# The last 32 adaLN blocks as float32 matmuls on TensorE, moved to other places, and activation tiles of 1 KB

## The chip, the cores and the metric

The kernel runs on one core of a Trainium2 chip. TensorE multiplies into PSUM (eight banks of 128 x 512 float32), VectorE and ScalarE work on PSUM and SBUF, GpSimd on SBUF, and SyncE issues the loads from memory. The time is device microseconds from launch to end, the median of several executions, and lower is better. A profiled execution gives the trace that is read below.

## The reference

One decoder block on 256 tokens of 1,024 channels: an adaLN modulation from a condition vector `c`, a normalisation, one wide input projection that feeds two mixers (native sparse attention and gated DeltaNet), their merge, an output projection, and a gated feed-forward with a short convolution. The part that the change touches is the first line:

```python
mod = (c @ w_ada[l] + b_ada[l])[:, None, :]              # 6 x 1024 numbers from c (1024)
sh_m, sc_m, gt_m, sh_f, sc_f, gt_f = jnp.split(mod, 6, axis=-1)
h = rms_norm(x, norm_mix[l]) * (1.0 + sc_m) + sh_m
q_a, kv_a, gl_a, qkv_b, a_b, b_b, z_b, merge = jnp.split(h @ w_in[l], split_at, axis=-1)
y_a = nsa_attention(q_a, ...)
y_b = gated_deltanet(qkv_b, a_b, b_b, z_b, ...)
mixed = g_a * (y_a @ w_proj_nsa[l]) + g_b * (y_b @ w_proj_gdn[l])
x = x + gt_m * (mixed @ w_out[l])
h = rms_norm(x, norm_ffn[l]) * (1.0 + sc_f) + sh_f
x = x + gt_f * ((jax.nn.silu(u_gate) * u_val) @ ffn_down[l])   # u: up-projection and conv of h
```

So `mod` is one matrix-vector product, 1,024 by 6,144. Its first third (sh_m, sc_m) is wanted at once; gt_m at the residual behind `w_out`, sc_f and shf at the second normalisation, gt_f at the very end.

## The kernel before, in words

Activations lie with channels on partitions, as eight pieces of 128 channels by 256 tokens. Every weight matrix comes in tiles of 128 x 1,024 float32 (512 KB) through five raw slots (tag `wraw`). Each is split: ScalarE casts it to `whi` (line 242), VectorE or GpSimd subtracts to get `wlo` (line 243). A projection `lin` takes two such tiles and makes 48 matmuls of 128 x 256, three for each of 16 products (lines 265, 267, 268), into one of three PSUM banks of tag `lin`.

The stages in program order: the modulated norm with the k and q projections of the DeltaNet (until about 100 us); the DeltaNet's preparation with v and query projections; keys, values and the compression for the attention, among them the z projections `gates_z`; the attention loop `scores` / `probs` / `trans` / `values` over 16 heads, beside which the delta rule's steps (`inverse`, `delta`) run; eight projections for the merge gates `mg`; eight output projections `pn` and `pg` of the two mixers; four of `w_out` (source tile `mxh`); and the feed-forward: `up` projections, convolutions, `down` matmuls (`dn`, lines 1127 to 1129).

The 6,144 numbers of `mod` are made in 48 blocks of 128. A block is one 512 KB load into a raw slot (line 209) and one VectorE instruction with a fused sum (line 213), which multiplies it with `c` spread over all partitions. Sixteen blocks stand in the first stage. The others are placed by the table `ADA`: a count for each z projection, each merge-gate projection, each output projection, one number for each `w_out` projection, and the first feed-forward step from which eight single blocks follow.

Apart from the very start (`manual_schedule`), the order of the instructions on each engine is made by a list scheduler when the program is built. It takes the program order as priority, simulates the engines, and lets a later stage's work move ahead wherever its inputs, its buffers and its engine are free; that is how projections come to lie among the attention's steps. Every tag is a ring of buffers: an instruction that writes a new tile waits for a free one. SyncE issues loads strictly in its order, so a load that waits for its slot holds the loads behind it. `big` makes the activation tiles of tag `b8`: eight pieces in one tile, two tiles in the ring (`hh` and `hl`, then `mxh` and `mxl`, then `fh` and `fl`).

Of the kernel before, what the change touches and what calls it, by code (L numbers as in the profile page):

```python
# [12 lines left out]
F32R = mybir.dt.float32r  # L13
# [3 lines left out]
ALU = mybir.AluOpType  # L17
# [4 lines left out]
P = 128  # L22
D = 1024
KB = D // P
T = 256
# [20 lines left out]
QG = 1  # L46
ADA = ([0] * 4, [1] * 8, [1] * 8, 2, 4)
WARM = (2, 4)
# [4 lines left out]
for _name, _w in (("bada", 48), ("nmix", 8), ("nffn", 8), ("nfin", 8), ("conv", 96), ("fconv", 132),  # L53
                  ("fconvb", 44), ("gnorm", 1), ("ckb1", 2), ("cvb1", 2), ("ckb2", 1),
                  ("posk", 16), ("posv", 16), ("rows", 80)):
    COLS[_name] = (_n, _n + _w)
    _n += _w
# [44 lines left out]
def build(tc, a, probe=None):  # L102
    nc = tc.nc
    V, S, G, TE = nc.vector, nc.scalar, nc.gpsimd, nc.tensor
    with ExitStack() as ctx:
# [11 lines left out]
        def big(name):  # L117
            t = wk.tile([P, KB, T], F32R, name=name, tag="b8", bufs=2)
            return [t[:, k] for k in range(KB)]

# [33 lines left out]
        start = ExitStack()  # L154
# [57 lines left out]
        def adasum(m, w):  # L212
            V.tensor_tensor_reduce(w, w, cb, 1.0, cl("bada", m), ALU.mult, ALU.add, mod[:, m:m + 1])  # L213

        def ada(n=1):

            for _ in range(n):
                m = next(mods)
                adasum(m, adaload(m))

# [753 lines left out]
        for i in range(18):  # L974
            if i < 15:
                queries(i + 1)
            if i < 16:
                scores(*divmod(i, 4))
            if 1 <= i <= 16:
                probs(*divmod(i - 1, 4))  # L980
                if i % 4 == 0:
                    compressed(i // 4 - 1)
            if i >= 2:
                trans(*divmod(i - 2, 4))
                if i % 4 == 1:
                    values((i - 2) // 4)
# [196 lines left out]
def layout(x, c, w_ada, b_ada, norm_mix, w_in, nsa_pos_k, nsa_pos_v, nsa_ck_w1, nsa_ck_b1, nsa_ck_w2, nsa_ck_b2,  # L1183
# [8 lines left out]
    order = [b for k in range(8) for b in (8 + k, k)] + [*range(16, 24), *range(32, 40), *range(24, 32), *range(40, 48)]  # L1192
    wa = np.asarray(w_ada)[0].T.reshape(48, P, D)[order]
    d["ada"] = f(wa)
    ba = np.asarray(b_ada)[0].reshape(48, P)[order].T

    def pairs(w):
# [30 lines left out]
                                  chan(np.asarray(nsa_cv_b1)[0]), np.tile(np.asarray(nsa_ck_b2)[0], 2)[:, None],  # L1228
                                  pos(nsa_pos_k), pos(nsa_pos_v), np.broadcast_to(rows, (P, 80))], 1))
    d["const"] = constants()  # L1230
# [15 lines left out]
```

## Time and profile before

| | us |
|---|---|
| median of 3 runs | 658.89 (656.87 to 660.06) |
| profiled execution, its own time | 659.57 |
| its span, first to last instruction | 657.4 |
| TensorE busy | 594.0 |
| VectorE busy | 521.7 |
| ScalarE busy | 381.9 |
| GpSimd busy | 342.6 |

In the rows below PE is TensorE's matmuls, PEld its weight loads, DVE VectorE, ACT ScalarE, POOL GpSimd, SP SyncE. A row of a window gives its start and end in us, its length, then for each engine the busy time and in brackets the number of instructions, the granted TensorE clock (1.00 is full), the busy share of the DMA engines and the GB/s moved. A row of a group gives line, engine, operation, output and inputs by name, shapes and type, the count, then the busy time in us and the mean ns of one, and the idle time of the engine in front of it with what ended it. A float32 matmul is recorded as two passes.

### The profile page before, as it was taken

The page shows a single profiled execution, that of the slowest core. Times are in us where ns is not written, and L with a number is a line of the kernel's source. Part 1 is how long each engine was busy: PE and PEld are TensorE (multiplying, and loading weights), DVE is VectorE, ACT ScalarE, POOL GpSimd, SP SyncE. Part 2 cuts the span into 40 slices and gives each one's busy share as a digit, 9 for nine tenths or more (in the row PEclk, how much of TensorE's full clock was granted, in tenths as well). Part 3 has the DMA queues.
Part 4 walks back from the last instruction along what each step waited for, and adds up shares of the span by engine and source line. Part 5 has one row for each costly group of instructions (what it writes and reads, how often), then busy time and mean ns, then how long its engine had stood idle before and what let it go on. Part 6 is the DMA issues. An engine that isn't in the chain of part 4 may idle for free.

```text
span 657.4 us, 13689 instructions
## 1 busy us (share of the span) xinstructions
PE 594.0 (90%) x5128; PEld 560.1 (85%) x5128; DVE 521.7 (79%) x1209; ACT 381.9 (58%) x855; POOL 342.6 (52%) x239
## 2 busy tenths in 40 slices
PE   7888999899998988999899899698876989999994
PEld 4887899788998877999887898698866989999994
DVE  5989859789999998697967889779997577575645
ACT  4324997744565586596786542566554565555443
POOL 3324797735675777364622363456642276644431
PEclk9999999999998999899999999799996999999998
DMA  7788666344695644233432557764776556363501
GB/s 289 247 295 319 216 203 207 105 154 133 194 290 192 229 159 140 88 97 130 160 99 66 167 203 254 273 225 132 243 221 238 174 204 198 131 224 130 193 1 64
DMA packets 35363, 119.72 MB, mean 182 GB/s; under 512 B 4961, under 2 KB 5729, under 8 KB 35298
## 3 DMA queue, kind: packets, MB, share of 16 engines
q1 hardware_dynamic: 35298, 118.86, 53.7%
q8 instruction: 40, 0.66, 0.4%
q14 instruction: 25, 0.20, 0.1%
HBM read 117.66 MB, written 1.18 MB: 181 GB/s over the span
## 4 chain that ended last, share of the span: by engine, by line
PE 39%; DVE 34%; DMA 11%; ACT 7%; issue 5%; POOL 2%; SPq 1%; DVEq 0%; ACTq 0%; POOLq 0%
DMA wada<-in_ada 8%; PE lin L265 8%; PE lin L268 8%; PE lin L267 8%; DVE wada L213 7%; DVE wlo L243 5%; PE dn L1128 3%; PE dn L1129 3%; PE dn L1127 2%; ACT whi L242 2%; POOL wlo L243 2%; DVE pp L921 2%; DVE cacc L397 1%; DVE pp L905 1%; DVE fl L1101 1%
## 5 line engine op out<-in xcount | busy, mean ns | idle before, releaser
L243 POOL TENSOR_TENSOR wlo<-wraw,whi 128x1024 fp32r<-128x1024 f32 x90 | 230.4, 2569 | 177.1 <-ACT whi L242 84.5
L242 ACT CAST whi<-wraw 128x1024 fp32r<-128x1024 f32 x144 | 149.9, 1048 | 79.3 <-PE lin L267 23.6
L265 PE MATMUL lin<-hh,whi 128*128 128x256 f32 x384 | 112.0, 292 | 1.0 <-DVE cacc L397 0.7
L268 PE MATMUL lin<-hh,wlo 128*128 128x256 f32 x384 | 111.5, 291 | 0.0
L267 PE MATMUL lin<-hl,whi 128*128 128x256 f32 x384 | 111.4, 290 | 0.0
L213 DVE CUSTOM_DVE_ANT_0 wada<-wada,cb,col 128x1024 f32<-128x1024 f32 x48 | 84.8, 1768 | 15.3 <-DMA wada<-in_ada 15.3
L243 DVE TENSOR_TENSOR wlo<-wraw,whi 128x1024 fp32r<-128x1024 f32 x54 | 84.2, 1560 | 7.3 <-ACT whi L242 6.1
L265 PE MATMUL lin<-fh,whi 128*128 128x256 f32 x304 | 86.7, 286 | 3.0 <-DVE al L252 3.0
L267 PE MATMUL lin<-fl,whi 128*128 128x256 f32 x304 | 86.8, 286 | 1.8 <-DVE fl L1101 1.8
L268 PE MATMUL lin<-fh,wlo 128*128 128x256 f32 x304 | 86.7, 285 | 1.3 <-DVE wlo L243 1.3
L265 PEld LDWEIGHTS lin<-hh,whi 128*128 128x128 f32 x384 | 74.6, 194 | 1.9 <-ACT whi L242 0.8
L268 PEld LDWEIGHTS lin<-hh,wlo 128*128 128x128 f32 x384 | 74.6, 195 | 0.8 <-issue 0.3
L267 PEld LDWEIGHTS lin<-hl,whi 128*128 128x128 f32 x384 | 74.5, 194 | 0.6
L265 PEld LDWEIGHTS lin<-fh,whi 128*128 128x128 f32 x304 | 58.8, 194 | 3.4 <-DVE al L252 3.4
L267 PEld LDWEIGHTS lin<-fl,whi 128*128 128x128 f32 x304 | 58.9, 194 | 2.3 <-DVE fl L1101 2.3
L268 PEld LDWEIGHTS lin<-fh,wlo 128*128 128x128 f32 x304 | 58.9, 194 | 1.5 <-DVE wlo L243 1.5
L243 POOL TENSOR_TENSOR dlo<-wraw,dhi 128x1024 fp32r<-128x1024 f32 x14 | 36.1, 2583 | 44.9 <-ACT dhi L242 42.3
L1127 PE MATMUL dn<-ah,dhi 128*128 128x256 f32 x176 | 48.4, 285 | 6.2 <-ACT ah L251 6.2
L1128 PE MATMUL dn<-al,dhi 128*128 128x256 f32 x176 | 49.7, 284 | 3.7 <-DVE al L252 3.7
L1129 PE MATMUL dn<-ah,dlo 128*128 128x256 f32 x176 | 49.1, 281 | 0.0
L1127 PEld LDWEIGHTS dn<-ah,dhi 128*128 128x128 f32 x176 | 33.2, 193 | 6.9 <-ACT ah L251 6.8
L1128 PEld LDWEIGHTS dn<-al,dhi 128*128 128x128 f32 x176 | 34.0, 193 | 4.4 <-DVE al L252 4.4
(410 smaller groups left out, 1608.3 us busy)
## 6 DMA issues: line engine op xcount, KB each, us to landing
wraw<-in_win SPq DMA_DIRECT2D x52, 512.0 KB, 3.7
wada<-in_ada SPq DMA_DIRECT2D x48, 512.0 KB, 4.5
wraw<-in_up SPq DMA_DIRECT2D x44, 512.0 KB, 4.3
wraw<-in_down SPq DMA_DIRECT2D x22, 512.0 KB, 4.0
wraw<-in_wko SPq DMA_DIRECT2D x16, 512.0 KB, 5.3
wraw<-in_pn SPq DMA_DIRECT2D x8, 512.0 KB, 4.2
wraw<-in_pg SPq DMA_DIRECT2D x8, 512.0 KB, 3.7
wraw<-in_wo SPq DMA_DIRECT2D x8, 512.0 KB, 4.1
```

Source lines behind the costliest of these rows:

```text
L213: V.tensor_tensor_reduce(w, w, cb, 1.0, cl("bada", m), ALU.mult, ALU.add, mod[:, m:m + 1])
L242: recent[S] = S.copy(hi, w).ins
L243: recent[e] = e.tensor_tensor(lo, w, hi.bitcast(F32), op=ALU.subtract).ins
L265: TE.matmul(o[:, b], hi[:, j, cs], hh[k], start=k == 0 and b == 0, stop=False, skip_group_check=True)
L267: TE.matmul(o[:, b], hi[:, j, cs], hl[k], start=False, stop=False, skip_group_check=True)
L268: TE.matmul(o[:, b], lo[:, j, cs], hh[k], start=False, stop=k == KB - 1 and b == blocks - 1, skip_group_check=True)
L397: V.scalar_tensor_tensor(acc[:, sft:], src[:, :T - sft], col[:, w0 + 3 - sft:w0 + 4 - sft], acc[:, sft:], op0=ALU.mult, op1=ALU.add)
L905: V.tensor_tensor_reduce(ap[0], src, ap[1], 0.125, -3e38, ALU.add, ALU.max, mx[:, 1 + w, t, r:r + 1])
L921: (G if 2 * w + t in POOLP else V).tensor_scalar(pv, pv, wt[:, 1 + w, t, r:r + 1], None, op0=ALU.mult)
L1127: TE.matmul(o, hi[:, cs], ah, start=f == 0 and b % 2 == 0, stop=False, skip_group_check=True)
L1128: TE.matmul(o, hi[:, cs], al, start=False, stop=False, skip_group_check=True)
L1129: TE.matmul(o, lo[:, cs], ah, start=False, stop=f == NF - 1 and b % 2 == 1, skip_group_check=True)
```

## The change

Blocks 16 to 47 are no longer summed by VectorE. `adapart` multiplies a block on TensorE in eight float32 matmuls: the stationary operand is one column of `c` spread over 32 columns, the moving one a 128 x 128 piece of the block, and the output goes to one of four strips of 32 partitions, each strip taking two of the eight. ScalarE copies the 128 x 128 result to SBUF, a second float32 matmul with a selecting column adds the four strips and turns the row into a column, and VectorE adds the bias. The bank is one of the three of tag `lin`; the copy `adt` lies in the ring `th` (16 buffers), which the delta rule's steps use too. On the host the weights of those 32 blocks are transposed, and nine columns (`c` and the selector) join the constants.

The places change as well: one block behind each head's `scores` (16), none at the merge gates and at `w_out`, eight at the output projections and eight in the feed-forward as before. And `big` makes eight tiles of 1 KB per partition with 16 in the ring, where it made one of 8 KB with two.

```diff
--- before.py
+++ after.py
@@ -44,7 +44,7 @@
 PARTS = 2
 OUTS = {0: 0, 1: 1, 3: 2, 5: 4, 7: 6}
 QG = 1
-ADA = ([0] * 4, [1] * 8, [1] * 8, 2, 4)
+ADA = ([0] * 4, [0] * 8, [1] * 8, 0, 4)
 WARM = (2, 4)
 GC = math.sqrt(2.0 / math.pi)
 
@@ -52,7 +52,7 @@
 _n = 0
 for _name, _w in (("bada", 48), ("nmix", 8), ("nffn", 8), ("nfin", 8), ("conv", 96), ("fconv", 132),
                   ("fconvb", 44), ("gnorm", 1), ("ckb1", 2), ("cvb1", 2), ("ckb2", 1),
-                  ("posk", 16), ("posv", 16), ("rows", 80)):
+                  ("posk", 16), ("posv", 16), ("rows", 80), ("cc", 8), ("sel", 1)):
     COLS[_name] = (_n, _n + _w)
     _n += _w
 NCOLS = _n
@@ -115,8 +115,7 @@
             return ps.tile(list(shape), F32, name=name, tag=tag, bufs=PB[tag])
 
         def big(name):
-            t = wk.tile([P, KB, T], F32R, name=name, tag="b8", bufs=2)
-            return [t[:, k] for k in range(KB)]
+            return [wk.tile([P, T], F32R, name=name, tag="b8", bufs=16) for _ in range(KB)]
 
         TAGS = {"mg": (46, 256), "ma": (24, 256), "mz": (24, 256), "tc": (8, 256), "tg": (10, 256), "ta": (4, 256),
                 "th": (16, 128), "t2": (3, 512), "yf": (3, 512), "qq": (2, 512), "lb": (4, 1024), "mk": (2, 1024), "mf": (1, 1024), "dh": (8, 1024), "t4": (6, 1024)}
@@ -216,7 +215,18 @@
 
             for _ in range(n):
                 m = next(mods)
-                adasum(m, adaload(m))
+                (adapart if m >= 16 else adasum)(m, adaload(m))
+
+        def adapart(m, w):
+
+            o, t = bank("ad", "lin"), tl("adt", "th")
+            for k in range(KB):
+                q = 32 * (k % 4)
+                TE.matmul(o[q:q + 32, :P], cl("cc", k).to_broadcast([P, 32]), w[:, k * P:k * P + P], start=k < 4,
+                          stop=k >= 4, skip_group_check=True)
+            S.copy(t, o[:, :P])
+            TE.matmul(o[:, P:P + 1], t, cl("sel", 0), start=True, stop=True, skip_group_check=True)
+            V.tensor_tensor(mod[:, m:m + 1], o[:, P:P + 1], cl("bada", m), op=ALU.add)
 
         mods = itertools.count(2)
 
@@ -976,6 +986,7 @@
                 queries(i + 1)
             if i < 16:
                 scores(*divmod(i, 4))
+                ada()
             if 1 <= i <= 16:
                 probs(*divmod(i - 1, 4))
                 if i % 4 == 0:
@@ -1191,6 +1202,8 @@
 
     order = [b for k in range(8) for b in (8 + k, k)] + [*range(16, 24), *range(32, 40), *range(24, 32), *range(40, 48)]
     wa = np.asarray(w_ada)[0].T.reshape(48, P, D)[order]
+
+    wa[16:] = wa[16:].reshape(32, P, KB, P).transpose(0, 3, 2, 1).reshape(32, P, D)
     d["ada"] = f(wa)
     ba = np.asarray(b_ada)[0].reshape(48, P)[order].T
 
@@ -1226,7 +1239,8 @@
                                   chan(norm_final), conv, fcv, chan(np.asarray(ffn_conv_b)[0]),
                                   chan(np.asarray(gdn_norm)[0]), chan(np.asarray(nsa_ck_b1)[0]),
                                   chan(np.asarray(nsa_cv_b1)[0]), np.tile(np.asarray(nsa_ck_b2)[0], 2)[:, None],
-                                  pos(nsa_pos_k), pos(nsa_pos_v), np.broadcast_to(rows, (P, 80))], 1))
+                                  pos(nsa_pos_k), pos(nsa_pos_v), np.broadcast_to(rows, (P, 80)), chan(np.asarray(c)[0]),
+                                  (np.arange(P)[:, None] % 32 == 0).astype(np.float32)], 1))
     d["const"] = constants()
     return d
 
```

What the built program makes of it is shown at three places. In the new file the lines behind the new function have numbers 10 or 11 higher.

TensorE, right behind the last matmuls of the compression (`hp`), where the attention begins; `lin` is a projection's bank, here for z and the merge gates. Before:

```order
L809 MATMUL hp<-whi,mk_2880 128x256
L810 MATMUL hp<-wlo,mk_2880 128x256
L265 MATMUL lin<-hh,whi 128x256
L267 MATMUL lin<-hl,whi 128x256
L265 MATMUL lin<-hh,whi 128x256
L267 MATMUL lin<-hl,whi 128x256
L268 MATMUL lin<-hh,wlo 128x256
L265 MATMUL lin<-hh,whi 128x256
L267 MATMUL lin<-hl,whi 128x256
L268 MATMUL lin<-hh,wlo 128x256
L265 MATMUL lin<-hh,whi 128x256
L267 MATMUL lin<-hl,whi 128x256
```

And with the change; `ad` is a block's bank, `ht` belongs to the compression, `s` holds a head's scores:

```order
L819 MATMUL hp<-whi,mk_2894 128x256
L820 MATMUL hp<-wlo,mk_2894 128x256
L225 MATMUL ad<-wada,col 32x128 x22
L827 MATMUL ht<-cst,hs 128x64 x2
L904 MATMUL s_3515<-KS,qq 128x272 x2
L904 MATMUL s_3515<-KS,qq 128x16 x2
L225 MATMUL ad<-wada,col 32x128 x2
L904 MATMUL s_3516<-KS,qq 128x512 x2
L904 MATMUL s_3551<-KS,qq 128x272 x2
L904 MATMUL s_3551<-KS,qq 128x16 x2
L850 MATMUL ht<-w_709,xr 96x64 x2
L904 MATMUL s_3552<-KS,qq 128x512 x2
```

Three blocks (24 matmuls) stand where projections stood. From here to the end of the delta rule the new order has no row of `lin` on TensorE; the old one has 480 such matmuls of `hh` and `hl` and 48 of the first output projections among the same steps. In the new order thirteen more blocks follow the delta rule's last matmul, and then the 480.

ScalarE, in the attention: `pp` are the softmax's probabilities, `mg` the merge gates out of their bank, `whi` a weight tile's cast. Before, in the middle:

```order
L914 ACTIVATE pp,misc<-pp,misc 128x128
L914 ACTIVATE pp,misc<-pp,misc 128x256
L914 ACTIVATE pp,misc<-pp,misc 128x128
L914 ACTIVATE pp,misc<-pp,misc 128x256
L881 CAST qq<-qT_835 64x256 x2
L242 CAST whi<-wraw 128x1024
L914 ACTIVATE pp,misc<-pp,misc 128x128
L914 ACTIVATE pp,misc<-pp,misc 128x256
L914 ACTIVATE pp,misc<-pp,misc 128x128
L914 ACTIVATE pp,misc<-pp,misc 128x256
L997 ACTIVATE mg_4478<-lin 128x256
L997 ACTIVATE mg_4479<-lin 128x256
```

And with the change at the attention's end, where its first rows of `adt` stand; `vn` and `sq` are the last steps of the delta rule, `oT` its output:

```order
L717 COPY vn_2663<-d_2696 128x128
L717 COPY vn_2664<-d_2696 128x128
L727 ACTIVATE sq,misc<-oT_2671 128x128
L261 CAST ya_3498<-y 128x256
L261 CAST ya_3500<-y 128x256
L261 CAST ybh_5250<-yb 128x256
L727 ACTIVATE sq,misc<-oT_2671 128x128
L727 ACTIVATE sq,misc<-oT_2672 128x128 x2
L227 COPY adt<-ad 128x128 x3
L261 CAST ybh_5251<-yb 128x256
L261 CAST ybh_5252<-yb 128x256
L261 CAST ybh_5253<-yb 128x256
```

The first copy out of a block's bank stands behind the delta rule's last squares. No cast of a weight tile stands between the first `pp` and there.

SyncE, from the last loads of the compression (`cvw`) on. Before:

```order
L230 DMA wraw<-in_cvw 128x1024 x3
L230 DMA wraw<-in_win 128x1024 x6
L209 DMA wada<-in_ada 128x1024
L230 DMA wraw<-in_win 128x1024 x2
L209 DMA wada<-in_ada 128x1024
L230 DMA wraw<-in_win 128x1024 x2
L209 DMA wada<-in_ada 128x1024
L230 DMA wraw<-in_win 128x1024 x2
L209 DMA wada<-in_ada 128x1024
L230 DMA wraw<-in_win 128x1024 x2
```

And with the change:

```order
L240 DMA wraw<-in_cvw 128x1024 x3
L208 DMA wada<-in_ada 128x1024 x8
L150 DMA x_5987<-in_x 128x512 x2
L150 DMA x_5988<-in_x 128x512 x2
L208 DMA wada<-in_ada 128x1024 x8
L240 DMA wraw<-in_win 128x1024 x20
L240 DMA wraw<-in_pn 128x1024 x2
L208 DMA wada<-in_ada 128x1024
```

Sixteen block loads, with the second load of `x` between them, stand ahead of all 20 tiles for z and the merge gates, where they alternated with them one to two.

## Rows read from the trace of the kernel before

**Rows 1.** The page: span, busy time of two engines, chain by engine.

```profile
span 657.4 us, 13689 instructions
PE 594.0 (90%) x5128; PEld 560.1 (85%) x5128; DVE 521.7 (79%) x1209; ACT 381.9 (58%) x855; POOL 342.6 (52%) x239
...
PE 39%; DVE 34%; DMA 11%; ACT 7%; issue 5%; POOL 2%; SPq 1%; DVEq 0%; ACTq 0%; POOLq 0%
```

**Rows 2.** Windows by stage, from the attention on.

```profile
208.00:358.00 150.00, 138.67 (x1594) 125.37 (x1594) 127.39 (x460) 105.77 (x334) 85.10 (x99) 0.98 0.42 138
358.00:403.00 45.00, 42.52 (x363) 41.87 (x361) 40.24 (x67) 20.76 (x40) 22.03 (x9) 1.00 0.57 188
403.00:425.00 22.00, 15.80 (x100) 14.32 (x101) 17.46 (x26) 7.29 (x9) 6.85 (x3) 0.84 0.82 281
425.00:465.00 40.00, 36.82 (x298) 36.03 (x297) 34.48 (x56) 25.19 (x52) 24.73 (x14) 1.00 0.50 163
465.00:535.00 70.00, 57.01 (x435) 55.19 (x434) 55.36 (x75) 36.00 (x56) 31.82 (x13) 0.93 0.64 213
535.00:657.00 122.00, 113.97 (x962) 113.31 (x961) 73.11 (x119) 64.67 (x110) 53.42 (x22) 0.98 0.42 146
```

**Rows 3.** Windows of 10 us, in the attention and behind it.

```profile
225.00:235.00 10.00, 8.53 (x96) 7.96 (x96) 9.94 (x35) 7.29 (x23) 9.46 (x8) 1.00 0.54 191
255.00:265.00 10.00, 7.32 (x85) 4.98 (x83) 7.33 (x20) 5.39 (x18) 6.53 (x7) 0.85 0.51 160
265.00:275.00 10.00, 10.00 (x138) 9.52 (x137) 6.46 (x22) 3.75 (x11) 3.48 (x8) 0.81 0.18 54
295.00:305.00 10.00, 10.00 (x161) 8.70 (x160) 6.46 (x24) 4.44 (x14) 4.77 (x8) 1.00 0.46 159
375.00:385.00 10.00, 10.00 (x87) 9.89 (x86) 8.26 (x14) 5.66 (x9) 3.38 (x2) 1.00 0.51 165
405.00:415.00 10.00, 5.29 (x41) 4.68 (x39) 7.46 (x15) 3.68 (x5) 2.76 (x2) 1.00 0.86 302
```

**Rows 4.** The chain in order of time around 410 us: start, us, what.

```profile
402.94 3.33 DVE wada L213
...
409.27 5.49 DMA wada<-in_ada
...
414.88 1.28 DVE wada L213
```

**Rows 5.** Groups of TensorE by form, 208 to 358 us.

```profile
L268 PE MATMUL lin<-hh,wlo 128*128 128x256 f32 x159 | 46.5, 294 | 0.0
...
L265 PE MATMUL lin<-ya,whi 128*128 128x256 f32 x13 | 3.9, 301 | 0.0
```

**Rows 6.** VectorE's blocks: all of them (page), and those of 358 to 535 us.

```profile
L213 DVE CUSTOM_DVE_ANT_0 wada<-wada,cb,col 128x1024 f32<-128x1024 f32 x48 | 84.8, 1768 | 15.3 <-DMA wada<-in_ada 15.3
...
L213 DVE CUSTOM_DVE_ANT_0 wada<-wada,cb,col 128x1024 f32<-128x1024 f32 x20 | 37.9, 1897 | 9.1 <-DMA wada<-in_ada 9.1
```

**Rows 7.** Groups of VectorE by form, 208 to 358 us: blocks, weight splits.

```profile
L213 DVE CUSTOM_DVE_ANT_0 wada<-wada,cb,col 128x1024 f32<-128x1024 f32 x12 | 15.9, 1328 | 1.8 <-DMA wada<-in_ada 1.8
L243 DVE TENSOR_TENSOR wlo<-wraw,whi 128x1024 fp32r<-128x1024 f32 x10 | 14.7, 1472 | 0.2 <-ACT whi L242 0.2
```

**Rows 8.** DMA issues (page): count, KB of each, median us from issue to landing.

```profile
wada<-in_ada SPq DMA_DIRECT2D x48, 512.0 KB, 4.5
```

**Rows 9.** TensorE in order of time: start, us from first to last, what, count.

```profile
351.11 0.83 PE L697 MATMUL d<-St,kq 128*128 128x128 f32 x6
351.88 2.81 PE L967 MATMUL y<-pt,VV 128*64 128x256 f32 x30
```

**Rows 10.** Waits of TensorE, 375 to 560 us: total us, times, longest.

```profile
PE dn L1127 <- ACT ah L251: 6.2, 3, 3.9
PE lin L265 <- ACT mxh L251: 5.4, 3, 3.7
```

## The prediction

> **What bounds the kernel now.** I read the page first, then the stages one by one, the groups of instructions in two of them, and the waits and the chain last. Over the span TensorE is busy 90% and VectorE 79%, and both carry the chain of waits (39% and 34%) [rows 1]: neither is the bound alone, so the question is which of them limits which stage. The stages answer it [rows 2]. A projection runs at 87 matmuls in 10 us, 0.115 us each, with TensorE fully busy (375 to 385 in [rows 3]); that is the pace of a stage bound by TensorE. By it, 358 to 403 (363 matmuls, 42 of 45 us) and the tail from 535 (962, 111 of 122 us) are TensorE's. But 403 to 425 has 100 matmuls (11.5 us) in 22 us, and 465 to 535 has 435 (50 us) in 70 us: there TensorE waits, with VectorE busy 55.4 of 70 us, and the chain alternates between adaLN blocks, their loads and weight splits [rows 4]. The attention, 208 to 358, is of a third kind. Its matmuls are 475 of the merge-gate and z projections (three lines of 158 or 159, of which one is shown) and 39 of the first output projection (three lines of 13) [rows 5], laid between the steps of the softmax and of the delta rule. The attention's own chains leave holes; the projections fill them. In a slice such as 295 to 305 TensorE is at 10 of 10 and VectorE at 6.5; in 225 to 235 VectorE is at 9.9 [rows 3].
>
> **What the change does to the order.** The price lies here, less in the arithmetic. Taking a block off VectorE saves 1.77 us of it, 32 times, 57 us [rows 6]. But in the new order the first three blocks of the attention are multiplied ahead of everything, and each keeps one of the three banks of tag "lin" until ScalarE has copied it and VectorE has read the second product. ScalarE's first three copies stand behind the last square of the delta rule, at the attention's end. Every merge-gate and z projection needs a "lin" bank, so none can run in between. On SyncE the second blocks hold the five raw-weight slots as well, so nothing can be loaded ahead. All 480 projection matmuls of that kind follow the attention.
>
> **The terms**, against the profiled execution (span 657.4 us, time 659.57 us, so 2.2 us lie around it; the median 658.89 us is 0.1% below, which I ignore).
>
> *A. The attention without its filler.* The 514 matmuls leave the 150 us and cost 514 x 0.115 = 59 us elsewhere. What is left of VectorE there is 127.4 - 15.9 (blocks) - 14.7 (weight splits) = 96.8 us [rows 2, 7]; TensorE keeps about 139 - 59 = 80 us. At VectorE's present share of the stage (127.4 of 150, 85%) the rest takes 114 us; at the 99% of its best slice, 98 us. I take 110: near the first, as the delta steps still wait in turn, with a little off because TensorE's queue no longer holds foreign matmuls and GpSimd stops splitting weights. A = 110 + 59 - 150 = +19 us. The low end is 98, so +7. The high end: the granted clock fell to 0.81 in 265 to 275, after a slice with TensorE busy 7.3 of 10 [rows 3]; VectorE's work with all of today's idle time (22.6 us) is 119 us, and TensorE's 80 us become 99 at 0.81; if those 19 us come on top, the attention takes 138 us, +47.
>
> *B. Blocks that wait until the attention is over.* Thirteen remain; five lie loaded, eight of 512 KB must be fetched, then two raw tiles before a projection starts. At the best rate that this kernel shows, 302 GB/s [rows 3], a tile takes 1.74 us: ten tiles 17.4 us, and a first landing (4.5 us median [rows 8]) of which about half passes while the loaded blocks run. I take +20 us with little else on TensorE. Low end 12 us, TensorE's own work at 0.9 us a block; high end 26 us, if the three-bank rounds (products, copies, second products, additions) don't overlap with the loads, or the loads of x (1 MB, 3.5 us), which now stand between the two groups of eight blocks on SyncE, hold the second group back.
>
> *C. Eight blocks among the output projections*, a stretch that TensorE paces. What a block costs has to be bounded. Two strips of 64 columns run side by side in the value product: 3,072 columns of float32 in 2.8 us, 0.9 ns a column [rows 9]; a block's 8 x 128 columns would take 0.92 us. Four strips could halve that (0.46); a single one costs 0.11 us for each of two recorded passes of 128 columns (the first line of [rows 9]), so 1.8 us if the strips don't overlap. I take 0.9, the row that does the like: +7 us (4 to 14).
>
> The Trainium skill, "TensorEngine Tiling (Array Packing)", Key Properties, says that changing the tiling mode drains the engine. The rows don't show it: the first strip product starts at 351.88 us, before the modelled end of the full-width products ahead (351.11 + 0.83) [rows 9]. By the rule, with a drain of one 0.28 us matmul, two switches for each of 16 blocks would add an estimated 9 us to C and E; by the rows, nothing, and the sum goes by the rows.
>
> *D. The wait ahead of the w_out projection.* 403 to 425 loses 22 - 11.5 = 10.5 us; the chain there is a block (3.3 us), a block's load (5.5) and another block (1.3) [rows 4]. TensorE waits for mxh, 5.4 us [rows 10]; a part stays, as mxh's last pieces need the last projection. -7 us (-3 to -9).
>
> *E. The start of the feed-forward.* 425 to 465 gives back some 1 us (0 to 3). 465 to 535 loses 20 us; VectorE's eight blocks there cost it some 15 us at the 1.9 us mean of that part of the kernel [rows 6], and TensorE's waits for ah, 6.2 us, follow from its lag [rows 10]. I give back 11 (5 to 14), since the convolutions stay. The eight blocks now cost TensorE 8 x 0.9 = 7 us (4 to 14).
>
> *Nothing* for the rest. The 1 KB tiles let mxh or fh be written piece by piece as hh or mxh is released; but mxh's first piece comes after the merge-gate projections anyway, and fh waits for the norm's sum over all of w_out. A gain is bounded by D's wait (5.4 us), a loss by nothing larger than one release. The nine extra constant columns ride in a load that is there. The three blocks ahead of the attention (2.8 us) take the place of 36 projection matmuls (4.1 us) that stood ahead of the first scores. The copies on ScalarE and the additions of one column on VectorE lie beside TensorE's work: ScalarE is busy 20.8 of 45 us among the output projections, 36 of 70 in the feed-forward's start [rows 2].
>
> Sum: 19 + 20 + 7 - 7 - 1 - 11 + 7 = +34 us; 657.4 + 34 + 2.2 = 694 us.
>
> **Rivals.**
> 1. *A milder loss*: the attention falls to VectorE's floor, loads and blocks overlap, four strips run at once, and VectorE's relief is given back in full. All low ends together are 7 + 12 + 4 - 9 - 3 - 14 + 4 = +1, so 661 us; halfway to my sum it is 677 us. For it: VectorE's 9.9 slices. Against: the delta steps' waits, and slots that are freed one by one.
> 2. *A dearer one*: TensorE at a low clock through the emptier attention and strips that don't overlap. With A +47, B +26, C and E's blocks 14 each, and the rest as taken (-7 - 1 - 11) the sum is +82, 742 us; it begins where half of that excess is there, at 717 us. For it: the 0.81 clock. Against: TensorE keeps 80 us of work there, and two strips did overlap. The Trainium skill, "TensorE: Matmul & The Clock Gate", Part 1, has the gate close on idleness; no row here has so thin an attention.
> 3. *Faster*: VectorE's relief decides. Its place is everything behind the attention and the attention itself, where blocks and GpSimd's splits slow its other work (a block takes 1.33 us there and 1.90 us later [rows 6, 7]). With the other terms at their good ends (12 + 4 - 9 - 3 - 14 + 4 = -6), the kernel wins from the point where the attention takes less than 150 - 59 + 6 = 97 us, just under today's 96.8 us of VectorE work. At 90 us it gives 652 us. Against: every term has to come out well at once, and 80 us of TensorE work sit in the same chains.
>
> **How the numbers follow.** Forecast 0.63 (677 to 717), rival 1 0.18, rival 2 0.12, rival 3 0.07. Rival 1 lies almost wholly above 662 us, so slower by over 0.5% (what a measurement of this kernel can tell from no change, about 3 us) gets 0.89, within it 0.05, faster 0.06. The range leaves out rival 3, the low end of rival 1 and most of rival 2: 669 to 722 us.
>
> **What would show it.** In the new profile: no projection on TensorE between the first strip products and the end of the delta rule; ScalarE's copies of "ad" starting only there; almost no DMA traffic through the attention, then a burst; an attention of 100 to 120 us; some 20 us of thin TensorE work; ten projections in a row at 0.115 us a matmul. The w_out stage should lose its load chain. I am wrong if the copies come early on the chip, if the attention still takes 130 us or only 90, or if a block in the feed-forward takes far from 0.9 us.

## The result, and the profile after

The changed kernel takes 690.26 us (median of 4 runs, 688.26 to 691.43) against 659.38 us for the kernel before: 1.0474 times as long, interval 1.0439 to 1.0510. Forecast were 694 us. First the page of its profiled execution: span, busy time by engine, the clock and the DMA share in 40 slices of 17 us (in tenths), the chain by engine.

```profile
span 686.5 us, 14886 instructions
...
PE 635.3 (93%) x5704; PEld 591.0 (86%) x5704; DVE 454.5 (66%) x1177; ACT 391.5 (57%) x887; POOL 328.1 (48%) x239
...
PEclk9999999999996698899799999999899999999998
DMA  7788554345752000026856555763665866554301
...
PE 60%; DVE 19%; ACT 9%; DMA 8%; issue 3%; SPq 1%; DVEq 0%; ACTq 0%
```

VectorE lost 67 us of work, and its share of the chain fell from 34% to 19% [rows 1]; TensorE's rose from 39% to 60%. Slices 13 to 18 are the attention: hardly any DMA traffic in slices 14 to 17, and a lower clock at its start (it is granted at 0.50 or at 1.00; a value between is a mean over a stretch). The stages by windows: attention in three parts (its sum is the last row), blocks that waited, merge-gate and z projections, output projections, w_out, its end, feed-forward.

```profile
204.80:245.00 40.20, 33.88 (x431) 26.91 (x431) 32.65 (x156) 24.44 (x87) 17.64 (x36) 0.70 0.12 41
245.00:280.00 35.00, 29.81 (x362) 24.06 (x360) 28.75 (x146) 28.77 (x111) 17.28 (x34) 0.90 0.01 2
280.00:311.70 31.70, 29.25 (x341) 23.21 (x339) 23.61 (x112) 24.48 (x94) 8.77 (x15) 0.90 0.15 52
311.70:332.80 21.10, 14.77 (x252) 11.26 (x250) 8.07 (x41) 10.55 (x37) 2.18 (x1) 0.87 0.74 275
332.80:392.30 59.50, 59.50 (x483) 59.50 (x484) 15.86 (x21) 28.94 (x44) 32.00 (x14) 0.96 0.63 213
392.30:445.20 52.90, 52.90 (x517) 50.41 (x519) 20.34 (x41) 20.80 (x33) 24.65 (x10) 1.00 0.63 219
445.20:469.00 23.80, 23.80 (x212) 23.60 (x213) 15.11 (x26) 16.12 (x32) 10.90 (x8) 1.00 0.56 190
469.00:487.80 18.80, 17.89 (x147) 17.63 (x147) 13.99 (x23) 10.74 (x21) 8.88 (x6) 1.00 0.53 183
487.80:686.50 198.70, 185.09 (x1598) 180.91 (x1596) 121.89 (x200) 108.03 (x180) 90.52 (x37) 0.97 0.48 168
204.80:311.70 106.90, 92.94 (x1129) 74.17 (x1128) 85.01 (x409) 77.69 (x290) 43.69 (x85) 0.82 0.09 31
```

Beside [rows 2], with the borders that the same instructions have in either trace (last product of the compression, last of the delta rule, first and last output projection, first fh projection):

| stage | before | after | difference |
|---|---|---|---|
| up to the attention | 207.4 | 204.8 | -2.6 |
| attention | 150.1 | 106.9 | -43.2 |
| blocks that waited | 0 | 21.1 | +21.1 |
| its projections, behind it | 0 | 59.5 | +59.5 |
| output projections | 45.1 | 52.9 | +7.8 |
| w_out, up to the first fh | 51.3 | 42.6 | -8.7 |
| feed-forward | 203.5 | 198.7 | -4.8 |
| span | 657.4 | 686.5 | +29.1 |

The lock shows at the attention's end: on ScalarE (start, us, what) the copies of the first three blocks stand behind the delta rule's last squares. Their products were made some 107 us earlier.

```profile
313.15 0.29 ACT L727 ACTIVATE sq<-oT 128x128 f32<-128x128 f32 x1
...
313.45 0.57 ACT L227 COPY adt<-ad 128x128 f32<-128x128 f32 x3
```

On TensorE from there (in brackets the idle time ahead and who ended it) come second products of three blocks, strips of the next three, and so on; then loads pace (the last wait, 2.45 us, is for copies that stand on ScalarE behind a weight cast, which waits for its load), until the first projection:

```profile
313.74 0.83 PE L228 MATMUL ad<-col,adt 128*128 128x1 f32 x6 [0.82 <-ACT adt L227]
314.50 1.52 PE L225 MATMUL ad<-wada,col 128*32 128x128 f32 x48
...
327.07 0.72 PE L225 MATMUL ad<-wada,col 128*32 128x128 f32 x16 [1.34 <-DMA wada<-in_ada]
...
332.70 0.58 PE L275 MATMUL lin<-hh,whi 128*128 128x256 f32 x1
```

SyncE's queue explains these loads: three raw slots asked for at the start, then nothing of weights until the burst. Most of the time in between the queue stood at the second load of `x`, in one wait (the last row: total us, times, longest).

```profile
204.86 3.13 SPq L208 DMA_DIRECT2D wada<-in_ada  x3
293.35 12.74 SPq L150 DMA_DIRECT2D x<-in_x  x4
306.13 16.39 SPq L208 DMA_DIRECT2D wada<-in_ada  x8
323.24 11.17 SPq L240 DMA_DIRECT2D wraw<-in_win  x7
...
SPq L150 <- DVE pt L940: 79.7, 1, 79.7
```

### The profile page after: what moved, and what is told of

It is laid out like the page before. It is cut to its first block, busy times and chain, and to the rows that moved or that the text cites. A ratio compares the mean times of both kernels' runs of the same rounds, so it can differ in the third digit from the quotient of the medians.

```text
span 686.5 us, 14886 instructions
## 1 busy us (share of the span) xinstructions
PE 635.3 (93%) x5704; PEld 591.0 (86%) x5704; DVE 454.5 (66%) x1177; ACT 391.5 (57%) x887; POOL 328.1 (48%) x239
## 4 chain that ended last, share of the span: by engine, by line
PE 60%; DVE 19%; ACT 9%; DMA 8%; issue 3%; SPq 1%; DVEq 0%; ACTq 0%
PE lin L275 13%; PE lin L277 13%; PE lin L278 13%; DMA wada<-in_ada 5%; DVE wada L212 3%; ACT pp L924 3%; PE dn L1138 3%; PE dn L1140 3%; PE dn L1139 3%; PE y L977 2%; PE ad L225 2%; DMA wraw<-in_win 2%; DVE wlo L253 2%; ACT whi L252 1%; DVE cacc L407 1%
## 5 line engine op out<-in xcount | busy, mean ns | idle before, releaser
L253 POOL TENSOR_TENSOR wlo<-wraw,whi 128x1024 fp32r<-128x1024 f32 x90 | 222.0, 2474 | 223.5 <-ACT whi L252 101.6
L275 PE MATMUL lin<-hh,whi 128*128 128x256 f32 x384 | 111.2, 290 | 1.0 <-DVE cacc L407 0.7
L253 DVE TENSOR_TENSOR wlo<-wraw,whi 128x1024 fp32r<-128x1024 f32 x54 | 76.5, 1417 | 46.1 <-PE lin L278 42.1
L893 POOL TENSOR_TENSOR qq<-qT,qq 64x256 fp32r<-64x256 f32 x32 | 23.8, 744 | 27.1 <-ACT qq L891 25.7
L212 DVE CUSTOM_DVE_ANT_0 wada<-wada,cb,col 128x1024 f32<-128x1024 f32 x16 | 32.1, 2011 | 2.8 <-DMA wada<-in_ada 2.5
```

Of the source, the lines that this page charges most:

```text
L253: recent[e] = e.tensor_tensor(lo, w, hi.bitcast(F32), op=ALU.subtract).ins
L275: TE.matmul(o[:, b], hi[:, j, cs], hh[k], start=k == 0 and b == 0, stop=False, skip_group_check=True)
L893: (G if QG else V).tensor_tensor(q[d, 1], src, q[own, 0].bitcast(F32), op=ALU.subtract)
```

## The experiments

Eleven kernels; each time stands beside runs of the kernel before on the same chip.

**1. A ring of its own for the copies.** In the changed kernel the copy `adt` shares the sixteen buffers of `th` with the delta rule; here it gets three of its own.

```diff
-  "th": (16, 128), "t2": ...
+  "th": (16, 128), "ad": (3, 128), "t2": ...
-  o, t = bank("ad", "lin"), tl("adt", "th")
+  o, t = bank("ad", "lin"), tl("adt", "ad")
```

> The changed kernel with one edit: the copy adt has a ring of its own (3 buffers) and no longer shares the delta rule's ring. Theory (lockout): the loss comes from the three 'lin' banks, held through the attention because ScalarE's copies waited for a buffer of the delta rule's ring. In the new order the copies come at once and projections lie in the attention again. The changed kernel spends 108.6 us in the attention, 19.3 us on the remaining blocks and 59.6 us on 480 projection matmuls, 187.5 us. With them interleaved TensorE has some 80 + 59 us plus 16 blocks at 0.75 us, about 151 us, and a few us of holes: 157 us, so a time of about 660 us (650 to 670). Rival (the moved blocks themselves: their loads ahead of the projections' weights and their TensorE work cost the loss, whenever they are copied): within 5 us of 690 us. The first 16 block loads still stand ahead of all projection weights, so the first projection should not start before about 30 us into the attention under either.

Measured: 658.31 us, ratio 0.9999 [0.9973, 1.0025]. The projections are back in the attention (114 of the 480 matmuls still follow it), and the whole loss is gone. So the order that the shared ring brings costs the 32 us, and the blocks on TensorE as such cost, on balance, what they bring. Windows of this kernel: two parts of the attention, the whole of it, and the time to the last output projection.

```profile
204.80:245.00 40.20, 39.79 (x617) 30.31 (x617) 32.06 (x166) 32.51 (x103) 24.27 (x39) 1.00 0.70 239
245.00:280.00 35.00, 33.28 (x451) 30.07 (x446) 29.60 (x104) 23.95 (x82) 20.87 (x28) 1.00 0.30 105
...
205.80:345.80 140.00, 136.19 (x1735) 116.82 (x1734) 107.30 (x437) 105.15 (x340) 71.94 (x97) 1.00 0.40 137
345.80:413.30 67.50, 67.50 (x640) 65.18 (x639) 31.22 (x71) 31.66 (x61) 30.14 (x13) 1.00 0.61 208
```

TensorE is nearly full (136.2 of 140.0 us in the attention) and VectorE has idle time: the bound has moved. TensorE's busy time over the span is 620.1 us against 594.0 before, its idle time 37.0 against 63.4: the 26 us that VectorE's relief gave back went into the 32 blocks, at 0.8 us each.

**2. The 1 KB tiles alone**, in the kernel before.

```diff
-  t = wk.tile([P, KB, T], F32R, name=name, tag="b8", bufs=2)
-  return [t[:, k] for k in range(KB)]
+  return [wk.tile([P, T], F32R, name=name, tag="b8", bufs=16) for _ in range(KB)]
```

> The kernel before with the 1 KB activation tiles alone. The changed kernel reached the attention 2.6 us earlier than the kernel before. Theory A (nothing): the tiles change no wait, and the 2.6 us are scatter between executions: ratio 0.998 to 1.002. Theory B: with separate tiles a matmul of one piece waits only for that piece, which helps the first stage, where TensorE waited for hh 4.1 us: ratio 0.994 to 0.997 and the first projection of the q heads about 2 us earlier (71 against 73 us).

Measured: 659.65 us, ratio 1.0022 [1.0002, 1.0042]. They do nothing of use.

**3. The new places with all blocks on VectorE** (and the weights of all blocks in their old layout).

```diff
-  (adapart if m >= 16 else adasum)(m, adaload(m))
+  adasum(m, adaload(m))
```

> The changed kernel's places and tiles, but all 48 blocks stay one VectorE instruction (the weights in their old layout). Theory (lockout by banks): a block holds no PSUM bank here, so the projections stay in the attention and the loss disappears: 655 to 670 us, the attention somewhat longer than before because 16 blocks fall into its start, and the wait ahead of w_out shorter. Rival (the places alone, 16 block loads ahead of the projections' weights, starve TensorE): 680 us or more.

Measured: 671.64 us, ratio 1.0202 [1.0170, 1.0233], between the two theories. The places alone cost 13 us in all, and the loss sits at one spot: 200 to 230 us in this kernel,

```profile
200.00:215.00 15.00, 6.66 (x42) 5.96 (x41) 14.30 (x44) 2.64 (x8) 3.06 (x2) 0.73 0.94 346
215.00:230.00 15.00, 10.09 (x41) 8.56 (x42) 15.00 (x38) 9.07 (x25) 13.75 (x13) 0.50 0.86 298
```

and in the kernel before:

```profile
200.00:215.00 15.00, 14.64 (x110) 14.65 (x111) 14.07 (x45) 8.22 (x14) 8.69 (x4) 0.89 0.45 167
215.00:230.00 15.00, 13.62 (x110) 12.94 (x109) 14.87 (x53) 8.84 (x23) 12.33 (x16) 1.00 0.74 249
```

VectorE, full already, gets fourteen blocks there (18.2 us); TensorE makes 83 matmuls instead of 220. The block loads also stand ahead of the projections' weights, as the rival had it: ScalarE's first weight cast there waits for its load.

```profile
222.51 1.04 ACT L252 CAST whi<-wraw 128x1024 fp32r<-128x1024 f32 x1 [4.06 <-DMA wraw<-in_win]
```

The two go together here, since VectorE's blocks free the slots; no run separates them.

**4. The old places, on TensorE, with the ring of its own.** (Experiment 1 with this line:)

```diff
-  ADA = ([0] * 4, [0] * 8, [1] * 8, 0, 4)
+  ADA = ([0] * 4, [1] * 8, [1] * 8, 2, 4)
...
   scores(*divmod(i, 4))
-  ada()
```

> The changed kernel with the old places (one block at each merge-gate and each output projection, two at each w_out projection, eight in the feed-forward) and a ring of its own for adt. Theory: with the lockout gone what is left of the change is VectorE's relief (32 x 1.77 us) against 32 blocks at about 0.75 us on TensorE; the stalls ahead of w_out and at the start of the feed-forward shrink by the 9 and 5 us that the changed kernel showed, while the attention pays 8 x 0.75 us: 645 to 655 us. Rival (VectorE's relief is worth nothing, since TensorE paces): 660 to 670 us.

Measured: 664.45 us, ratio 1.0094 [1.0065, 1.0122]: TensorE is busy 621.9 us, about as in experiment 1. The projections run at either place. This kernel is slower than experiment 1 all the same (the two intervals lie apart): TensorE's longest wait from the attention on is now the second product's, for ScalarE's copy (total us, times, longest).

```profile
PE ad L228 <- ACT adt L227: 8.6, 6, 3.7
```

It is 2.4 us in experiment 1. The longest case shows why: the copy stands in ScalarE's order behind a cast that waits for its load, and the second product holds the projections behind it on TensorE.

```profile
424.53 1.04 ACT L252 CAST whi<-wraw 128x1024 fp32r<-128x1024 f32 x1 [3.14 <-DMA wraw<-in_wo]
...
425.76 0.26 ACT L227 COPY adt<-ad 128x128 f32<-128x128 f32 x1
...
426.07 1.03 PE L228 MATMUL ad<-col,adt 128*128 128x1 f32 x4 [3.65 <-ACT adt L227]
```

**5. The same with the shared ring.** The first TensorE block now comes in the middle of the attention, so only its later half is shut.

> The changed kernel with the blocks at the places of before; the copies adt still share the ring th with the delta rule. Beside it stands the run with old places and a ring of its own: 664.5 us. Theory (the shared ring shuts the projections out of the attention from the first block onward, and the price goes with how long they are shut out): here the first TensorE block is asked for at the middle of the attention, so only the later half of the projections moves out; between 664.5 and the changed kernel's 690: 672 to 682 us, with the lin<-hh matmuls running on behind the last d by some 25 us. Rival (the price of 32 us came from the early places together with the ring, and not from the lockout): the ring alone costs nothing here, 662 to 667 us. A third (any shut-out costs the whole): 685 to 692 us.

Measured: 662.68 us, ratio 1.0042 [1.0024, 1.0061]. My theory of a price that goes with the time of the lock fell. Windows of this kernel up to the last delta product, and of the projections behind it:

```profile
205.60:245.00 39.40, 37.16 (x435) 34.82 (x433) 35.83 (x133) 28.61 (x82) 30.65 (x38) 1.00 0.46 162
245.00:280.00 35.00, 34.17 (x501) 27.70 (x501) 28.19 (x127) 27.19 (x96) 19.58 (x30) 1.00 0.23 77
280.00:321.50 41.50, 35.51 (x406) 27.91 (x403) 33.55 (x166) 33.14 (x130) 14.07 (x27) 0.96 0.08 27
321.50:358.50 37.00, 37.00 (x360) 34.44 (x359) 15.43 (x37) 19.40 (x48) 13.88 (x6) 1.00 0.54 202
```

The attention takes 115.9 us and holds 240 projection matmuls (three lines of 80; 27.6 us at 0.115 us), all in its first 75 us. Without any it took 106.9. So 27.6 us of projections, beside three blocks as in the changed kernel, lengthened it by 9: most of them went into slack, though they came early and not all along. That the amount of slack is fixed is argued from this, not shown.

**6, 7. Useless work in the slack.** To see whether the clock (granted 0.82 on average in the attention) or the empty slack is the price, the changed kernel got matmuls that nobody uses ahead of each of 32 groups of transposes, six or three.

```diff
   tp = bank("ptp", "at")
+  for _ in range(6):
+      TE.matmul(tp[:, :T], hh[1][:, :P], hh[0], start=True, stop=True, skip_group_check=True)
```

> The changed kernel, in which the attention runs without projections; ahead of each of the 32 groups of transposes of the probabilities stand six matmuls of 256 columns whose result is written over and used by nobody (32 x 6 x 0.115 us = 22 us of TensorE at the full clock). They give the attention back work of TensorE without giving it any work done. Theory (the lockout's 32 us are about half idle TensorE, 108.6 - 93.9 = 14.7 us, and about half the lower granted clock, mean 0.83, at which the attention's own matmuls take longer): the clock in the attention rises to 0.95 or more and useless work makes the kernel faster, 674 to 686 us, attention 94 to 104 us. Rival (the price is the missing overlap alone, or the matmuls stand in the chain): 690 to 712 us, attention 109 us or longer, whatever the clock.

> As the run with six matmuls ahead of each group of transposes, with three (11 us at the full clock). Theory of the clock: the gain comes with the clock that it restores, so between the changed kernel and the run with six, or as good as that one with less work in the way: 674 to 690 us. Rival (each matmul only adds to the chain): above the changed kernel, by half of what six add.

Measured: with six 696.12 us, ratio 1.0578 [1.0535, 1.0621]; with three 692.45 us, 1.0495 [1.0450, 1.0540], beside the changed kernel's 1.0474 (with three, no difference beyond the intervals). The attention with six:

```profile
206.30:317.50 111.20, 104.09 (x1323) 88.94 (x1322) 86.24 (x411) 77.89 (x290) 44.02 (x85) 0.95 0.09 30
```

The clock rose to 0.95, and the attention became no shorter (111.2 against 106.9 us): the theory of the clock, by which it would have taken 94 to 104, fell. The lower clock came with the emptiness. What it costs by itself is not separated here: the useless matmuls stand among the attention's own and may add to its chain what the clock gives back. And 22 us of useless matmuls (192 at 0.115) lengthened the attention by 4 us, at the higher clock: most of them fell into slack. TensorE's own work there is 104.1 us at 0.95 less those 22, or 92.9 at 0.82, some 76 us at the full clock by either (an estimate, with the mean clock of the window). So of 106.9 us about 30 could hold other work at the full clock, and the changed kernel leaves them empty. That is about the lock's price, by estimate. The traces of the changed kernel and of experiment 1 split it: the same 5,704 matmul records keep TensorE busy 635.3 and 620.1 us, at a mean clock of 0.952 and 0.985, and its idle time is 51.2 and 37.0 us.

**8. Sixteen blocks on TensorE**, the later ones (32 to 47), the others on VectorE; old places, ring of its own.

```diff
-  (adapart if m >= 16 else adasum)(m, adaload(m))
+  (adapart if m >= 32 else adasum)(m, adaload(m))
```

> The places of before, the ring of its own for adt, but only blocks 32 to 47 (output projections' end and feed-forward) on TensorE; the sixteen of the attention are back on VectorE. Theory (in the attention TensorE paces and a block on it costs 0.75 to 0.8 us, 12 to 13 us for sixteen; later VectorE paces and its relief gives that back or more): 664.5 less 12 or 13, 650 to 655 us. Rival (VectorE's 25 us of blocks in the attention cost as much there as TensorE's 12, since the two take turns): 660 to 666 us.

Measured: 662.60 us, ratio 1.0063 [1.0037, 1.0089]: the rival. The first sixteen (at the old places eight of them stand in the attention and eight among the output projections, so my sentence on them was wrong) are worth about as much on either engine: 1.0063 here and 1.0094 in experiment 4, with overlapping intervals.

**9. The gate's blocks later, all on VectorE.** The kernel before, with one number changed.

```diff
-  ADA = ([0] * 4, [1] * 8, [1] * 8, 2, 4)
+  ADA = ([0] * 4, [1] * 8, [1] * 8, 2, 12)
```

> The kernel before with one number changed: the last eight blocks (the feed-forward's gate) start at step 12 of the feed-forward instead of step 4; all 48 stay on VectorE, none on TensorE. Theory (VectorE's blocks are worth taking away only where VectorE ends last, 403 to 425 and 465 to 535 us, and a place with idle VectorE time is worth as much as TensorE without its 0.8 us a block): what TensorE idles in 465 to 535 because of these blocks comes back, 650 to 656 us. Rival (the blocks only shift the stall to the later steps, since every step of the feed-forward gives VectorE about the same work): 657 to 660 us. On the other side (the gate comes too late for the last steps, which then wait): 661 to 670 us.

Measured: 657.38 us, ratio 0.9947 [0.9915, 0.9979]; a small gain, at the rival's time. TensorE makes 504 matmuls in 465 to 535 us instead of 435, and 467 in 535 to 600 instead of 554: the eight blocks stand there now.

**10. Both**: only blocks 32 to 39 on TensorE, the last eight on VectorE from step 12.

> As the run with blocks 32 to 47 on TensorE, but only 32 to 39 there (the eight that stand ahead of w_out's merge, where VectorE is the last to end); the last eight back on VectorE and from step 12 of the feed-forward. Theory: the eight on TensorE pay (VectorE's 14 us of blocks in 403 to 425 against 6 us of TensorE) and the late eight cost TensorE nothing: 644 to 651 us, below the kernel before by over 1%. Rival (the eight on TensorE cost as much as they free, so that only the late gate counts): equal to the run that changes the late gate alone, within 2 us. Other side: the last steps wait for the gate, over 660 us.

Measured: 659.27 us, ratio 0.9986 [0.9965, 1.0007]; no gain is seen, though the interval just overlaps that of experiment 9. Even where VectorE was last to end, eight blocks on TensorE didn't pay in this order; 6.0 us of TensorE's waits in 400 to 463 us are the second products' for ScalarE's copies, as in experiment 4.

**11. The gate's blocks at every second step**, all on VectorE, in the kernel before.

```diff
-  if ADA[4] <= f < ADA[4] + 8:
+  if ADA[4] <= f < ADA[4] + 16 and f % 2 == 0:
```

> The kernel before, with the last eight blocks (the feed-forward's gate) at every second step of the feed-forward, 4 to 18, instead of at eight steps in a row from 4; all on VectorE. The run with the eight in a row from step 12 is at 0.9947 [0.9915, 0.9979] of before: TensorE is full there in 495 to 535 us, but loses 8 us in 535 to 600 us, where they now stand. Theory (a block every second step fits beside VectorE's weight work, a block at each step doesn't): the stall nearly goes, 645 to 653 us. Rival (the stall belongs to the steps and not to the number of blocks in a row): 655 to 660 us.

Measured: 650.71 us, ratio 0.9888 [0.9850, 0.9926]: faster than both kernels by more than the interval. Windows of this kernel:

```profile
465.00:535.00 70.00, 62.91 (x500) 61.82 (x499) 51.73 (x71) 41.63 (x62) 36.93 (x15) 0.95 0.66 220
535.00:600.00 65.00, 65.00 (x555) 65.00 (x554) 43.97 (x74) 36.60 (x60) 34.90 (x14) 1.00 0.61 204
```

In 465 to 535, 500 matmuls fit instead of 435 [rows 2], and 535 to 600 stays full (554 and 555). The feed-forward takes 195.9 us (452.6 to 648.5): 7.6 less than before, 2.8 less than the changed kernel's, without moving any work off VectorE. Its blocks got quicker too, 1.63 us each instead of 1.77 [rows 6]. That comes from the eight of the feed-forward: the rows are all 48 in this kernel, then those eight (450 to 660 us) before and in this kernel.

```profile
L213 DVE CUSTOM_DVE_ANT_0 wada<-wada,cb,col 128x1024 f32<-128x1024 f32 x48 | 78.2, 1630 | 15.5 <-DMA wada<-in_ada 15.4
...
L213 DVE CUSTOM_DVE_ANT_0 wada<-wada,cb,col 128x1024 f32<-128x1024 f32 x8 | 18.5, 2317 | 2.6 <-DMA wada<-in_ada 2.6
...
L213 DVE CUSTOM_DVE_ANT_0 wada<-wada,cb,col 128x1024 f32<-128x1024 f32 x8 | 10.7, 1332 | 3.6 <-DMA wada<-in_ada 3.6
```

## Why the prediction was right, point by point

*The order* was read rightly and is shown by experiments 1 and 5: three banks held, ScalarE's copies last, no projection in the attention, no weight traffic.

*A, +19; measured +20.9* (106.9 - 150.1, +59.5 for the merge-gate and z projections, +4.6 for the 39 of the first output projection). The length, 110 us, was right to 3 us; its reason was not. I worked it out from 96.8 us of VectorE work at 88%. VectorE had 85.0 us: instructions that are in both kernels took less time where GpSimd had no weights to split. One of them by form, 204.8 to 313.4 us, before (fewer of them, since the stage was longer):

```profile
L921 DVE TENSOR_SCALAR pp<-pp,misc 128x256 f32<-128x256 f32 x22 | 12.6, 574 | 0.3
```

and after:

```profile
L931 DVE TENSOR_SCALAR pp<-pp,misc 128x256 f32<-128x256 f32 x32 | 12.5, 390 | 0.2
```

The mean of 574 ns hides what happened. Two of the 22 took 2.52 and 2.13 us; the other 20 make 0.40 us each. Each of the two lies beside a split on GpSimd and ends behind it; the second, with its split:

```profile
253.88 2.13 DVE L921 TENSOR_SCALAR pp<-pp,misc 128x256 f32<-128x256 f32 x1
...
253.48 2.38 POOL L243 TENSOR_TENSOR wlo<-wraw,whi 128x1024 fp32r<-128x1024 f32 x1
```

VectorE was at 80% (85.0 of 106.9 us), and the share of an engine was the wrong measure. TensorE's waits there are spread over GpSimd, ScalarE and VectorE; the first three of the list (total us, times, longest):

```profile
PE ptp L939 <- POOL pp L931: 4.4, 3, 2.4
PE pa L674 <- ACT x L668: 1.1, 2, 0.6
PE s L904 <- DVE xg L834: 1.0, 1, 1.0
```

It reads as a chain of short steps over four engines: the largest parts of the chain that ended last in 204.8 to 311.7 us are ScalarE's `pp` (18.1%), TensorE's `y` (12.7%) and VectorE's `pp` (5.7%). 27.6 and 22 us of further work on TensorE lengthened it by 9 and 4 us (experiments 5 and 6). The projections cost 59.5 + 4.6 = 64 us instead of 59: 480 of them at 0.124 us, at a clock of 0.96. So the attention came out 3 us below my figure and the projections 5 above it: that A fits to 2 us is in part luck.

*B, +20; measured +21.1*, at 275 GB/s; I had taken 302.

*C, +7; measured +3.2* (7.8 less the 4.6 us of moved matmuls). A block among projections costs the 0.9 us that I took, though not as I took it. Its strips hold the projections up by 0.66 us (445.69 less 444.91 in the rows, less the 0.12 that projections lie apart),

```profile
444.91 0.28 PE L278 MATMUL lin<-ybh,wlo 128*128 128x256 f32 x1
445.12 0.64 PE L225 MATMUL ad<-wada,col 128*32 128x128 f32 x16
445.69 0.38 PE L275 MATMUL lin<-mxh,whi 128*128 128x256 f32 x1
```

and its second product, which I had not priced, by two records, 0.23 us. Seven of the eight lie ahead of the last output projection's end, 6.2 us; some 2.5 us of that fit into what TensorE had idled there before (42.5 of 45 us busy, [rows 2]). (The row that I took for the price, [rows 9], is 15 products, 16 records of 256 columns and 14 of 128: 2,944 columns and not 3,072, 4% off.)

The Trainium skill, "TensorEngine Tiling (Array Packing)", Key Properties, has a drain at each change of the mode. I had written that the rows don't show it, by the modelled end of the product ahead; that was the wrong sign to go by. By the starts they fit a small one, in all sixteen single blocks among projections: 0.21 us from the last projection to the first strips and 0.20 us from the last strips back, where projections lie 0.12 apart. So a switch costs about 0.09 us, and 32 of them some 3 us and not the 9 that I had estimated; without its two switches a block's strips take 0.48 us, so the four do overlap, as the low bound had it.

*D, -7, and E's first term, -1, which lies mostly in the same stretch; measured -8.7.* *The rest of E, -4; measured -4.8.* The sum was 5 us high; 2.6 of that is the stretch ahead of the attention, which I had at nothing. It varies as much from kernel to kernel: with the small tiles alone it ended at 204.5 us in a kernel that gained nothing.

*The rivals.* Rivals 1 and 3 both needed an attention near 97 us by VectorE's floor; with 85.0 us of VectorE work it still took 106.9, so that floor doesn't set it. And VectorE's relief, on which rival 3 rested, decided nothing even without the lock: experiment 1 gains 26 us of TensorE's idle time and spends 26. Rival 2's clock did fall (0.70 in the first 40 us), but the attention didn't get the 28 us longer that it priced; its strips did overlap. The Trainium skill, "TensorE: Matmul & The Clock Gate", Part 1, has the gate close on idleness: the trace agrees (0.82 with the thin attention, 0.95 with useless matmuls, 1.00 with the projections of experiment 1), but the attention's time didn't follow the clock in the runs with useless matmuls.

That experiment 5, with the shared ring, is not slower than experiment 4, without (1.0042 and 1.0094), fits TensorE's waits for ScalarE's copies, 1.7 and 8.6 us; no run takes these waits away. What stays open: what the lower clock costs by itself in the attention; where the 1.7 us ahead of the attention in the run with six useless matmuls come from; and what else than the eight blocks keeps 465 to 535 at 62.9 of 70 us in experiment 11.

## What to carry to other kernels

Before moving work to a "free" engine, count what the engine that paces would idle less, and what it must do more: here 26 us and 26 us. A buffer ring that a helper shares with a long chain can lock out everything that needs the helper's other buffers; look in the new order for what holds a bank, and for how long. A product that waits for another engine's copy holds everything behind it in its own engine's order, as in experiment 4. Where two engines collide in one stretch, spacing the work out on the same engine can be worth more than moving it: one block every second step gave 1.1%, moving them to TensorE nothing.

## What the runs showed of the hardware

- Four strips of 32 columns in float32 run at once: in the changed kernel their records start in fours, 6 to 7 ns apart (from 314.50 us on), and each lasts 0.27 to 0.30 us. So 24 matmuls of 128 columns take 1.52 us, 0.063 us each, where one over the full width costs two records of 0.11 us [rows 9].
- A change between projections over the full width and strips costs about 0.09 us either way: starts 0.21 and 0.20 us apart where they are 0.12 apart otherwise (444.91 to 445.69 us; the other fifteen single blocks among projections are within 0.01 us of it). No run separates it from the load of the strips' weights.
- VectorE's 128x256 scaling took 2.13 and 2.52 us where it ran into a weight split of GpSimd (2.38 us), and 0.40 us otherwise. The Trainium skill, "GPSIMD Engine Reference", section 1 (Specifications), has the two engines share their interfaces to SBUF, with contention for some of VectorE's instructions; the trace agrees for this one.
- The granted clock over the first 40 us of the attention was 0.70, and 0.87 with six useless matmuls ahead of each group of transposes; the attention took 106.9 and 111.2 us. These runs don't separate what the clock gave back from what the useless matmuls cost.
